# Banded attention scores: the correction product over all 128 rows, and the fp32 scores of two heads in turn

## The chip, the cores and the metric

One core of a Trainium2 chip runs the whole program. The metric is the time of one execution on the device in microseconds: a median of 1695.29 us over three runs (1690.89 to 1697.64).

## What is computed

The reference is an encoder trunk of two layers over 512 tokens of 1024 features, all in float32. The first layer mixes tokens by attention with 16 heads of 64 features, the second by a state-space layer; after each comes a gated feed-forward of 2816 hidden features, and a norm ends the trunk. The change concerns the attention alone. It has three groups of queries, keys and values (a window of 128 tokens; 512 with dilation 4; 2048 with dilation 16), whose outputs are weighted by a softmax over their log-sum-exps:

```python
scores = jnp.einsum('brnqhe,brnkhe->brnhqk', qb, kw, preferred_element_type=jnp.float32)
scores = jnp.where(valid[None, None, :, None], scores + bias[None, None, None], NEG_INF)
m = jnp.max(scores, axis=-1, keepdims=True)
p = jnp.exp(scores - m)
den = jnp.sum(p, axis=-1, keepdims=True)
o = jnp.einsum('brnhqk,brnkhe->brnqhe', p, vw.astype(jnp.float32))
o = o / den.transpose(0, 1, 2, 4, 3, 5)
lse = (m + jnp.log(den))[..., 0].transpose(0, 1, 2, 4, 3)
...
weights = jax.nn.softmax(jnp.stack(lses, axis=0), axis=0)
o = jnp.sum(weights[..., None] * jnp.stack(outs, axis=0), axis=0)
```

## The kernel before

**Main products.** A weight block of 128 x 1024 is loaded by a DMA that SP issues (L91) three blocks ahead, and split into a high part by ACT (L111) and the rest by DVE (L112). A product of 512 columns is then three matmuls for each of 8 feature tiles (high by high, high by low, low by high) in PSUM (`gemm_a`, L735; for the values of the second and third group `emit_v`, L836, with 256 columns). A pair p of heads (2p and 2p + 1, on partitions 0 to 63 and 64 to 127) has seven such units: q1, k1, q2, k2, q3, k3 and v1. `plan` gives their order: pairs one after another, with a block of values before pairs 1, 3, 5 and 7.

**The steps of attention** are put between the matmuls of later units. `bg.span` gets a list of steps, each with a cost in ns, and the main work of the span in ns (216 a matmul). After each feature tile, `bg.tick` adds 648 times the ratio of the two sums (and 1.02) to a credit, and issues the next step when the credit has reached half its cost, which is then taken off. So the order on each engine's queue is fixed when the program is written. The lists come from `A`, `W`, `B`, `mix`, `scores` and `values` (L998 to L1018): for an even head h, `scores(h)` has the four score steps of h, and those of h + 1 among the weighting steps of h; `values(h)` has the transposes and the products with the values of both heads. `spans` (L1020) sets them over the units: pairs 0, 1, 3 and 5 get scores and values over the q/k units of the pair behind them, pairs 2, 4 and 6 get their scores over a block of values, and `A(14)` lies over the very last unit. Head 15 and the values of the last pair stand in `tailp` (L1062), whose first five steps are issued while the operand of the output projection is made (`xo`, ACT L1059 and DVE or POOL L1060), and the rest between the matmuls of that projection (L1079, L735).

**Score steps.** `sc1(h, bp)` (L866) makes the banded scores of two blocks of 128 queries against 256 keys each. The keys' tile of a head holds their high part in one half of the partitions and their low part in the other; QA or QB holds the queries' high part in both halves. So one matmul over 128 rows (L880) gives high by high and high by low; a second (L881) adds the queries' low part QL by the keys' high part, over the head's 64 rows alone:

```python
nc.tensor.matmul(ps[:, j, :], QQ[:, b * 128:(b + 1) * 128], kap(KK), start=True, stop=False)
nc.tensor.matmul(ps[:, j, :], QL[rows, b * 128:(b + 1) * 128], kap(KK[rows]), start=False, stop=True)
```

`sc2(h, rp)` (L889) makes the scores of the other two groups, in fp32, over the head's 64 rows: four matmuls of 128 columns (L898, L899). Each step writes one bank of the PSUM pool `pss`, which has two. DVE reads a step's result with two instructions that add the distances, scale and take the maximum (L884 or L902); ACT then takes the exponential (L913).

**Weighting and values.** `weigh` has four parts (16 small copies on POOL, L925, then DVE and ACT); `tr` transposes on PE (L954, L959), with the result split by ACT and DVE (L962, L963); `pv` multiplies with the values (L978, L989) and ends a head with t1 (ACT L992, DVE L993, L994).

Where the parts of the queries are made (`qk_out`), QL is one tile per pair with two buffers; DVE writes its halves at L782 and L783. At the start of the program two small tiles `grow` receive the norms' gains by DMA, `sqd` takes squares of the input, of which only the sums are used, and t1 has a tile of 64 partitions with two buffers.

Of the kernel before, what the change touches and what calls it, by code (L numbers as in the profile page):

```python
# [13 lines left out]
P = 128  # L14
S = 512
# [11 lines left out]
def consts():  # L27
    """Tables that depend on shapes alone."""
    i = np.arange(128)
    q = np.arange(128)  # L30
    # natural tile: partition (r, i'), token 128 b + 4 i' + r
    d1 = np.full((128, 3, 2, 4, 32), BIG, np.float32)
    starts = {0: (0, 16), 1: (16, 48), 3: (80, 96)}
    for v, b in enumerate((0, 1, 3)):
        tq = 128 * b + 4 * (q % 32) + q // 32
        for T in range(2):
            for r in range(4):
                j = np.arange(32)
                tk = 4 * (starts[b][T] + j) + r
                dist = np.abs(tq[:, None] - tk[None, :])  # L40
                ok = dist <= 64
                if b == 0 and T == 0:
                    ok = ok & (j < 16)[None, :]
                if b == 3 and T == 1:
                    ok = ok & (j >= 16)[None, :]
                d1[:, v, T, r, :] = np.where(ok, dist, BIG)
    di = np.abs(i[:, None] - i[None, :])
    d2 = np.where(di <= 64, 4 * di, BIG)
    d3 = np.where(di % 4 == 0, 4 * di, BIG)
    dist = np.concatenate([d1.reshape(128, 768), d2, d3], axis=1).astype(np.float32)  # L50
    qs = np.zeros((128, NH // 2), np.float32)
    for p in range(NH // 2):
        qs[:64, p] = -1.0 / (8.0 * SLOPES[2 * p])
        qs[64:, p] = -1.0 / (8.0 * SLOPES[2 * p + 1])
    part = np.arange(128)
    dmask = (part[:, None] % 32 == np.arange(16)[None, :]).astype(np.float32)
    return np.concatenate([dist, qs, np.eye(128, dtype=np.float32), dmask], axis=1).astype(np.float32)
# [9 lines left out]
def fv(ap):  # L67
    return ap.bitcast(F32)


class WStream:
    """Weight blocks of [128, <=1024], loaded ahead and split into two f32r parts."""
# [22 lines left out]
    def split_to(self, n):  # L95
        nc = self.k.nc
        while self.ns <= min(n, len(self.units) - 1):
            w = self.raw.pop(self.ns)
            a, b = w.shape[1], w.shape[2]
            hi = self.pool.tile([P, 1024], F32R, tag="whi", name="whi")  # L100
            lo = self.pool.tile([P, 1024], F32R, tag="wlo", name="wlo")
            hv, lv = (t[:, 0:a * b] for t in (hi, lo))
            wv = w.rearrange("p a b -> p (a b)")
            if self.ns in self.swap:
                # columns (g, c) become (c, g)
                src = w.rearrange("p a (g c) -> p a c g", c=16)
                h4, l4 = (t.rearrange("p (a c g) -> p a c g", a=a, c=16) for t in (hv, lv))
                nc.scalar.activation(out=h4, in_=src, func=ACTF.Copy)
                self.lo_engine.tensor_tensor(out=l4, in0=src, in1=fv(h4), op=ALU.subtract)
            else:  # L110
                nc.scalar.activation(out=hv, in_=wv, func=ACTF.Copy)  # L111
                self.lo_engine.tensor_tensor(out=lv, in0=wv, in1=fv(hv), op=ALU.subtract)  # L112
            self.hl[self.ns] = tuple(t.rearrange("p (a b) -> p a b", a=a) for t in (hv, lv))
            self.ns += 1
# [9 lines left out]
class Bg:  # L124
    """Work put between the matmuls of the main products."""
# [27 lines left out]
class Cycle:  # L153
    """Tiles from several pools in turn."""
# [10 lines left out]
class Later:  # L165
    """An engine whose instructions are written down, to be issued in parts."""
# [9 lines left out]
class Tables:  # L176
    """What the state-space layer needs of its parameters, on the chip: rows are (direction, state)."""
# [15 lines left out]
    def scratch(self, n, cols):  # L193
        """A tile that is needed only while the parameters are worked out."""
        if not self.spare:
            tag, size = self.tags.pop()
            t = self.pool.tile([P, size], F32, tag=tag, name="sp_" + tag)
            self.spare = [t[:, i:i + 512] for i in range(0, size - 511, 512)]
        return self.spare.pop()[:, 0:cols]
# [4 lines left out]
    def cmul(self, eng, o_r, o_i, ar, ai, br, bi, t, neg=False):  # L204
        """o = a * b; neg gives -imag."""
# [8 lines left out]
    def exp(self, x, out, em1=None):  # L214
        """exp(x), and exp(x) - 1, to float32's accuracy."""
# [22 lines left out]
    def sincos(self, x, s, c, cm1):  # L238
        """sin, cos and cos - 1 of x, [128, 448]."""
# [46 lines left out]
    def params(self):  # L286
# [24 lines left out]
        # powers 1 .. 8 of lambda  # L311
# [6 lines left out]
        # f = (lambda - 1) / a  # L318
# [22 lines left out]
        for i in range(2):  # L341
# [4 lines left out]
            # the other direction from the far end  # L346
# [45 lines left out]
    def bc(self, w, i, g0):  # L392
        """powers [l, i, g] as (g, l, c)"""
# [3 lines left out]
    def ch(self, x):  # L397
        """channels (g, c) as (g, l, c)"""
# [73 lines left out]
    def store_e(self, T, s):  # L472
        # row (lam, c) of the block Toeplitz matrix is a window of the band at 16 lam
# [5 lines left out]
    def pieces(self):  # L479
        """(share of the time, what to issue)"""  # L480
# [32 lines left out]
def build(tc, a, out):  # L513
# [6 lines left out]
    # ---- weights in the order in which they are used  # L520
# [41 lines left out]
    # row 256 * t2 + 128 * tp + 64 * gp + s of w_glu: partition (tp, s), block (t2, gp)  # L562
# [13 lines left out]
    with ExitStack() as ctx:  # L576
# [19 lines left out]
        def norm_tile(pool, i, m, src_psum=None):  # L596
            """Parts of (gain * h)^T for feature tile m."""
# [9 lines left out]
        # of -y / 2 as an integer, the bits of a first guess at 1 / sqrt(y)  # L607
        GUESS = 1597463007.0 - 2.0 ** 22 - 2.0 ** 30

        def rs_col(ms, r):  # L610
            """r = rsqrt(ms / D + eps), [128, 4]"""
# [17 lines left out]
        # =================== attention ===================  # L629
# [12 lines left out]
        grow = [ap_.tile([8 * n, P], F32, name=f"grow{n}") for n in (1, 3)]  # L642
# [14 lines left out]
        # a first use of the exponential, so that its table is there  # L657
# [21 lines left out]
        def squares(c, act):  # L679
            for r in range(4):  # L680
                sqd = ap_.tile([P, 256], F32, tag="sqd", name="sqd")
# [63 lines left out]
        def emit_qk(p, lo_, hi_):  # L745
            if lo_ == 0:
                qk[p] = {}
            for kind in ("q1", "k1", "q2", "k2", "q3", "k3", "v1")[lo_:hi_]:
                if p == 0 and kind == "q1":
                    # the scale of the tokens comes later  # L750
# [12 lines left out]
        def qk_out(p, kind, ps):  # L763
            if True:
# [9 lines left out]
                elif kind == "q1":  # L774
                    t = ap_.tile([P, S], F32, tag="tq", name="tq", bufs=2)
                    nc.vector.tensor_tensor(out=br(t), in0=rb(ps), in1=rb(rsB), op=ALU.mult)
                    QA, QB, QL = (ap_.tile([P, S], F32R, tag=n, name=n, bufs=2) for n in ("QA", "QB", "QL"))
# [4 lines left out]
                    nc.vector.tensor_tensor(out=QL[0:64], in0=t[0:64], in1=fv(QA[0:64]), op=ALU.subtract)  # L782
                    nc.vector.tensor_tensor(out=QL[64:128], in0=t[64:128], in1=fv(QB[64:128]), op=ALU.subtract)  # L783
# [82 lines left out]
        def sc1(h, bp):  # L866
# [4 lines left out]
            QQ = (QA, QB)[e]  # L871
            ps = pss.tile([P, 2, 256], F32, tag="s", name="sps")
            for j in range(2):
                b = 2 * bp + j
                i0, step = win[b]
                rows = slice(64 * e, 64 * e + 64)
# [4 lines left out]
                nc.tensor.matmul(ps[:, j, :], QL[rows, b * 128:(b + 1) * 128], kap(KK[rows]), start=False, stop=True)  # L881
# [7 lines left out]
        def sc2(h, rp):  # L889
            c = head(h)  # L890
            p, e = h // 2, h % 2
            rows = slice(64 * e, 64 * e + 64)
            q = qk[p]
            ps = pss.tile([P, 2, 256], F32, tag="s", name="sps")
            for j in range(2):
                r = 2 * rp + j
                cs = slice(r * 128, (r + 1) * 128)
                nc.tensor.matmul(ps[:, j, 0:128], q["q2"][rows, cs], q["k2"][rows, cs], start=True, stop=True)  # L898
                nc.tensor.matmul(ps[:, j, 128:256], q["q3"][rows, cs], q["k3"][rows, cs], start=True, stop=True)  # L899
            for j in range(2):  # L900
                r = 2 * rp + j
                nc.vector.tensor_tensor_reduce(out=c.P2[:, r, :], in0=ps[:, j, :], in1=dist23,  # L902
                                               scale=-SLOPES[h], scalar=-3e38, op0=ALU.add, op1=ALU.max,
                                               accum_out=c.st[:, 4 + r:5 + r])
            fin(c, c.P2, 2 * rp, 4)

        # st: 0:8 m, 8:16 den, 16:24 partner m, 24:32 partner den (halves swapped), 32:40 -m, 40:48 work
# [8 lines left out]
        def weigh(h, part):  # L916
# [9 lines left out]
            elif part == 1:  # L926
                # par[.., k] holds the partner values of the other kind: slot k of par goes with slot 1-k of own
# [38 lines left out]
        def pv(h, t):  # L966
# [23 lines left out]
            if t == 1:  # L990
                t1 = ap_.tile([64, 2, 256], F32, tag="t1", name="t1", bufs=2)
# [6 lines left out]
        def A(h):  # L998
            return [(750, lambda: sc1(h, 0)), (880, lambda: sc2(h, 0)), (750, lambda: sc1(h, 1)), (880, lambda: sc2(h, 1))]
# [8 lines left out]
        def mix(x, y):  # L1008
            """the steps of two heads in turn"""
# [3 lines left out]
        def scores(h):  # L1013
            w, x = W(h), A(h + 1)
            return A(h) + [w[0], x[0], w[1], x[1], w[2], w[3], x[2], x[3]]
# [16 lines left out]
        def sq_add(m, acc):  # L1032
            """acc += h^2 for feature tile m."""
# [35 lines left out]
        for m in range(4):  # L1069
            wl = ws.get(ahead=min(1, 3 - m))  # L1070
            ps = (psg, psg, pss, pss)[m].tile([P, S], F32, tag="ggss"[m], name="aps")
            if m == 0:
                # the second parts of the operand come last
# [24 lines left out]
        # tables of the state-space layer, built between the products  # L1098
# [28 lines left out]
        # =================== feed-forward ===================  # L1127
        def ffn_in(hp, ep, psp, X, st, lo_, hi_, off, hid, pool_mult):
# [16 lines left out]
            for j in range(lo_, hi_):  # L1145
                gp = psp.tile([P, S], F32, tag="f", name="gps2")
                if st["rB"] is None and not late:
                    # the last feature tile of the input and the sums of squares come late
# [41 lines left out]
        for half in range(2):  # L1190
            ffn_in(hp0, e0, psf, Y, st, half * HALF, (half + 1) * HALF, half * HALF, hid, False)
            for m in range(KT):
# [6 lines left out]
                else:  # L1199
                    # from here on tokens lie as (l, j), t = 8 j + l  # L1200
# [15 lines left out]
        # =================== state-space layer ===================  # L1216
# [28 lines left out]
        def s_rho(T):  # L1245
            # decay per step, none across the ends of a group
# [189 lines left out]
        # =================== second feed-forward and last norm ===================  # L1436
# [102 lines left out]
```

## Time and profile before

| | |
|---|---|
| Median of three runs | 1695.29 us (1690.89 to 1697.64) |
| Profiled execution, first to last instruction | 1689.3 us |
| What the median has above that span | 6.0 us |
| Instructions | 22568 |
| Matmul engine (PE) busy | 1586.0 us, 94% |
| Weight loads (PEld) busy | 1287.1 us, 76% |
| DVE, ACT, POOL busy | 1015.5, 654.9, 528.7 us |
| Mean granted TensorE clock | 0.977 |

The profile has one execution. PE's busy time overlaps itself: a matmul's recorded length runs past the start of the next, so what a matmul costs is read from the distance of two starts. A weight load has a record of its own. "Idle before" an instruction names what ended the idle time, by the semaphore that came last; "issue" means that the profile shows no such cause. The attention stage runs to about 592 us, with the last unit of pair 7 at about 549 us.

### The profile page before, as it was taken

The numbers are of one execution on the slowest core, as the hardware profiler recorded it, in microseconds if no ns is written. First come the engines' busy times: TensorE is split into PE (matmuls) and PEld (weight loads), VectorE is DVE, ScalarE is ACT, GpSimd is POOL, SyncE is SP. The second block draws the span as 40 slices with busy tenths as digits, with TensorE's granted clock in tenths as the row PEclk, the third lists the DMA queues.
The fourth block names the chain that finished last, engine by engine and source line by source line (L and its number), as shares of the span: only waits on it lengthen the run. The fifth ranks groups of instructions, "written<-read, shape, count | busy, mean of one in ns | idle before, by whom it ended". The sixth has DMA issues, their size and how long they took to land. (4 is left out here: it accounts for less than half of the span.)

```text
span 1689.3 us, 22568 instructions
## 1 busy us (share of the span) xinstructions
PE 1586.0 (94%) x8428; PEld 1287.1 (76%) x8428; DVE 1015.5 (60%) x1714; ACT 654.9 (39%) x1148; POOL 528.7 (31%) x784
## 2 busy tenths in 40 slices
PE   8999999999999889988988889888699999999997
PEld 6877887887888668866666667667578888888886
DVE  6466565555655678887777785568945434433223
ACT  5355454454444523343444444422133323332222
POOL 0011011020120340298887996345412110111010
PEclk9999999999999999999999998989899999999999
DMA  6322222222222033345655544657723333233332
GB/s 186 91 63 63 63 78 60 75 63 75 75 58 80 26 84 100 97 126 162 176 145 168 143 127 147 226 165 242 205 76 94 94 100 100 88 89 107 105 100 63
DMA packets 278669, 185.17 MB, mean 110 GB/s; under 512 B 39424, under 2 KB 260768, under 8 KB 276512
## 3 DMA queue, kind: packets, MB, share of 16 engines
q1 hardware_dynamic: 278128, 183.13, 36.9%
q8 instruction: 66, 1.08, 0.3%
q10 hardware_dynamic: 432, 0.60, 0.1%
q14 instruction: 43, 0.35, 0.1%
HBM read 154.34 MB, written 27.26 MB: 108 GB/s over the span
## 5 line engine op out<-in xcount | busy, mean ns | idle before, releaser
L112 DVE TENSOR_TENSOR wlo<-wraw,whi 128x1024 fp32r<-128x1024 f32 (+1 forms) x234 | 304.0, 1302 | 184.5 <-ACT whi L111 183.1
L111 ACT ACTIVATE whi<-wraw 128x1024 fp32r<-128x1024 f32 x238 | 241.3, 1018 | 248.4 <-PE ops L1498 76.0
L735 PE MATMUL gps<-xhi,whi 128*128 128x512 f32 x792 | 322.7, 407 | 0.0
L735 PE MATMUL gps<-xhi,wlo 128*128 128x512 f32 x792 | 312.2, 394 | 0.8 <-DVE wlo L112 0.8
L735 PE MATMUL gps<-xlo,whi 128*128 128x512 f32 x792 | 311.7, 394 | 0.5 <-DVE xlo L602 0.5
L925 POOL COPY st<-st 32x4 f32<-32x4 f32 x256 | 66.0, 258 | 484.5 <-ACT P L913 475.8
L735 PEld LDWEIGHTS gps<-xhi,wlo 128*128 128x128 f32 x792 | 149.4, 189 | 34.8 <-DVE wlo L112 1.2
L735 PEld LDWEIGHTS gps<-xhi,whi 128*128 128x128 f32 x792 | 149.6, 189 | 31.6 <-issue 1.5
L735 PEld LDWEIGHTS gps<-xlo,whi 128*128 128x128 f32 x792 | 149.9, 189 | 26.7 <-DVE xlo L602 0.8
L735 PE MATMUL ups<-xhi,whi 128*128 128x512 f32 x352 | 140.9, 400 | 0.0
L735 PE MATMUL ups<-xhi,wlo 128*128 128x512 f32 x352 | 138.7, 394 | 1.0 <-DVE wlo L112 1.0
L735 PE MATMUL ups<-xlo,whi 128*128 128x512 f32 x352 | 138.6, 394 | 0.0
L913 ACT ACTIVATE P<-P,st 128x256 f32<-128x256 f32 x128 | 64.1, 501 | 88.3 <-DVE st L910 88.2
L1137 POOL TENSOR_TENSOR u<-u,g 128x512 f32<-128x512 f32 x22 | 28.4, 1290 | 214.1 <-DVE u L1135 202.2
L735 PEld LDWEIGHTS ups<-xhi,wlo 128*128 128x128 f32 x352 | 66.9, 190 | 15.8 <-DVE wlo L112 1.5
L735 PEld LDWEIGHTS ups<-xhi,whi 128*128 128x128 f32 x352 | 67.0, 190 | 15.6 <-issue 2.3
L1134 ACT ACTIVATE g<-g 128x512 f32<-128x512 f32 x44 | 27.8, 631 | 129.2 <-DVE g L1133 129.2
L735 PEld LDWEIGHTS ups<-xlo,whi 128*128 128x128 f32 x352 | 67.0, 190 | 13.2
L963 DVE TENSOR_TENSOR PT<-ptp,PT 128x512 fp32r<-128x512 f32 x64 | 44.0, 690 | 54.5 <-ACT PT L962 54.1
L836 PE MATMUL vps<-whi,xhi 128*128 128x256 f32 x256 | 75.1, 293 | 0.0
L735 PE MATMUL fps<-hh,whi 128*128 128x512 f32 x176 | 72.7, 413 | 0.0
L836 PE MATMUL vps<-wlo,xhi 128*128 128x256 f32 x256 | 72.2, 282 | 0.0
(319 smaller groups left out, 3312.2 us busy)
## 6 DMA issues: line engine op xcount, KB each, us to landing
wraw<-in_w_ffn_in SPq DMA_DIRECT2D x88, 512.0 KB, 3.8
wraw<-in_w_qkv SPq DMA_DIRECT2D x72, 512.0 KB, 3.6
wraw<-in_w_ffn_out SPq DMA_DIRECT2D x38, 512.0 KB, 4.0
BD<-B SPq DMA_DIRECT2D x16, 512.0 KB, 3.4
TinD<-Tt SPq DMA_DIRECT2D x16, 512.0 KB, 2.6
Ti<-TinD SPq DMA_DIRECT2D x8, 1024.0 KB, 7.2
Bt<-BD SPq DMA_DIRECT2D x8, 1024.0 KB, 8.1
wraw<-in_w_glu SPq DMA_DIRECT2D x64, 128.0 KB, 3.9
```

The source lines that it names most:

```text
L111: nc.scalar.activation(out=hv, in_=wv, func=ACTF.Copy)
L112: self.lo_engine.tensor_tensor(out=lv, in0=wv, in1=fv(hv), op=ALU.subtract)
L735: nc.tensor.matmul(dst, w[:, kt, :], x, start=(start and kt == ks[0] and j == 0), stop=(stop and kt == ks[-1] and j == 2))
L836: nc.tensor.matmul(ps[rp][:, r % 2, :], x, w[:, kk, :], start=(kt == 0 and j == 0 and r % 2 == 0), stop=(kt == 7 and j == 2 and r % 2 == 1))
L913: nc.scalar.activation(out=Pt[:, j, :], in_=Pt[:, j, :], func=ACTF.Exp, bias=st[:, 32 + off + j:33 + off + j], accum_out=st[:, 8 + off + j ...
L925: nc.gpsimd.tensor_copy(par[32 * z:32 * z + 32, y, :, :], own[32 * y:32 * y + 32, z, :, :])
L963: nc.vector.tensor_tensor(out=PT[:, 1, :], in0=ps, in1=fv(PT[:, 0, :]), op=ALU.subtract)
L1134: nc.scalar.activation(out=g, in_=g, func=ACTF.Silu)
L1137: eng.tensor_tensor(out=u, in0=u, in1=g, op=ALU.mult)
```

## The change

- The correction product of the banded scores (L881) uses all 128 rows. There are four QL tiles, made once: two for pairs in turn, two for the heads of a pair. Each is zero in the other head's half; POOL clears these halves at the start. DVE writes the head's own half as before.
- `sc2` takes a pair in place of a head. It takes both banks of `pss`, and issues the matmuls of the two heads in turn: q2 by k2 of head 0, of head 1, q3 by k3 of head 0, of head 1. DVE's readings follow, head by head.
- The lists: an even head's has sc1, sc2 of the pair, sc1, sc2 of the pair; an odd head's has its two sc1 alone. Costs are 600 for sc1 and 1200 for the pair's sc2, where they were 750 and 880.
- `grow`, `sqd` and t1 lie in one tile t1x of 128 partitions: t1 of a head in the head's 64 partitions, with one buffer. Comments and docstrings are taken out.

```diff
+        t1x = ap_.tile([P, 2, 256], F32, name="t1x")
+        t1f = t1x.rearrange("p a b -> p (a b)")
+        grow = [t1f[0:8, 0:128], t1f[0:24, 128:256]]
+        QLs = [[ap_.tile([P, S], F32R, name=f"QL{i}{e}") for e in range(2)] for i in range(2)]
+        for i in range(2):
+            for e in range(2):
+                nc.gpsimd.memset(QLs[i][e][64 * (1 - e):64 * (1 - e) + 64].bitcast(F32), 0.0)
...
-                sqd = ap_.tile([P, 256], F32, tag="sqd", name="sqd")
+                sqd = t1f[:, 256:512]
...
-                    nc.vector.tensor_tensor(out=QL[0:64], in0=t[0:64], in1=fv(QA[0:64]), op=ALU.subtract)
-                    nc.vector.tensor_tensor(out=QL[64:128], in0=t[64:128], in1=fv(QB[64:128]), op=ALU.subtract)
+                    nc.vector.tensor_tensor(out=QL[0][0:64], in0=t[0:64], in1=fv(QA[0:64]), op=ALU.subtract)
+                    nc.vector.tensor_tensor(out=QL[1][64:128], in0=t[64:128], in1=fv(QB[64:128]), op=ALU.subtract)
...
-                nc.tensor.matmul(ps[:, j, :], QL[rows, b * 128:(b + 1) * 128], kap(KK[rows]), start=False, stop=True)
+                nc.tensor.matmul(ps[:, j, :], QL[:, b * 128:(b + 1) * 128], kap(KK), start=False, stop=True)
...
+        def sc2(p, rp):
+            cc = [head(2 * p + e) for e in range(2)]
             q = qk[p]
+            pp = [pss.tile([P, 2, 256], F32, tag="s", name="sps") for e in range(2)]
             for j in range(2):
                 r = 2 * rp + j
                 cs = slice(r * 128, (r + 1) * 128)
+                for i, (nq, nk) in enumerate((("q2", "k2"), ("q3", "k3"))):
+                    for e in range(2):
+                        rows = slice(64 * e, 64 * e + 64)
+                        nc.tensor.matmul(pp[e][:, j, 128 * i:128 * i + 128], q[nq][rows, cs], q[nk][rows, cs],
+                                         start=True, stop=True)
+            for e, c in enumerate(cc):
+                for j in range(2):
...
+                fin(c, c.P2, 2 * rp, 4)
...
-                t1 = ap_.tile([64, 2, 256], F32, tag="t1", name="t1", bufs=2)
+                t1 = t1x[64 * e:64 * e + 64]
...
-            return [(750, lambda: sc1(h, 0)), (880, lambda: sc2(h, 0)), (750, lambda: sc1(h, 1)), (880, lambda: sc2(h, 1))]
+            s = [(600, lambda: sc1(h, 0)), (600, lambda: sc1(h, 1))]
+            t = [(1200, lambda i=i: sc2(h // 2, i)) for i in range(2)]
+            return s if h % 2 else [s[0], t[0], s[1], t[1]]
...
-            return A(h) + [w[0], x[0], w[1], x[1], w[2], w[3], x[2], x[3]]
+            return A(h) + [w[0], x[0], w[1], x[1], w[2], w[3]]
```

## Rows read from the trace of the kernel before

**Rows 1.** The page: span, and busy us (share) with instructions of each engine.

```profile
span 1689.3 us, 22568 instructions
...
PE 1586.0 (94%) x8428; PEld 1287.1 (76%) x8428; DVE 1015.5 (60%) x1714; ACT 654.9 (39%) x1148; POOL 528.7 (31%) x784
```

**Rows 2.** Busy time by stretches: PE, PEld, DVE, ACT, POOL, clock, DMA share, GB/s.

```profile
78.00:158.00 80.00, 80.00 (x387) 61.96 (x385) 50.47 (x146) 43.60 (x102) 12.43 (x50) 1.00 0.23 66
...
549.00:563.00 14.00, 10.47 (x42) 6.90 (x41) 11.59 (x28) 7.13 (x20) 10.76 (x21) 0.83 0.01 2
...
560.00:562.00 2.00, 2.00 (x9) 1.78 (x8) 2.00 (x3) 0.00 (x1) 2.00 (x3) 0.50 0.00 0
```

**Rows 3.** Timeline of PE, one step of banded scores: start us, us, instruction.

```profile
134.69 0.40 PE L735 MATMUL gps<-xhi,wlo 128*128 128x512 f32 x1
134.92 0.28 PE L880 MATMUL sps<-KA,QA 128*128 128x256 f32 x1
135.13 0.38 PE L881 MATMUL sps<-KA,QL 64*128 64x256 f32 x1
...
135.76 0.38 PE L881 MATMUL sps<-KA,QL 64*128 64x256 f32 x1
136.07 0.50 PE L735 MATMUL gps<-xhi,whi 128*128 128x512 f32 x1
136.41 0.39 PE L735 MATMUL gps<-xlo,whi 128*128 128x512 f32 x1
```

**Rows 4.** Timeline of PE, products of the values with 256 columns.

```profile
76.05 0.28 PE L836 MATMUL vps<-wlo,xhi 128*128 128x256 f32 x1
...
77.37 0.29 PE L836 MATMUL vps<-whi,xhi 128*128 128x256 f32 x1
```

**Rows 5.** Timeline of PEld, the load for the correction product.

```profile
135.13 0.18 PEld L881 LDWEIGHTS sps<-KA,QL 64*128 64x128 f32 x1 [0.25 <-issue]
```

**Rows 6.** Timeline of PE, one step of fp32 scores of one head.

```profile
80.85 0.40 PE L735 MATMUL gps<-xhi,wlo 128*128 128x512 f32 x1
81.17 0.48 PE L898 MATMUL sps<-k,q 64*128 64x128 f32 x2
81.50 0.38 PE L899 MATMUL sps<-k,q 64*128 64x128 f32 x2
...
81.95 0.38 PE L899 MATMUL sps<-k,q 64*128 64x128 f32 x2
82.26 0.50 PE L735 MATMUL gps<-xhi,whi 128*128 128x512 f32 x1
82.60 0.39 PE L735 MATMUL gps<-xlo,whi 128*128 128x512 f32 x1
```

**Rows 7.** The scores' PSUM tile by instruction: ns min/median/max, first and last start.

```profile
L898 PE MATMUL sps<-k,q x128: 268/272/579, 81.2 to 561.4; 64*128 64x128 f32 x128
...
L884 DVE CUSTOM_DVE_ANT_0 P<-sps,cst x64: 409/418/425, 81.6 to 563.3; 128x256 f32<-128x256 f32 x64
...
L880 PE MATMUL sps<-KA,QA x32: 278/334/386, 78.4 to 545.0; 128*128 128x256 f32 x32
```

**Rows 8.** Timeline of PE, state-space stage: products for two column halves in turn.

```profile
1116.51 0.70 PE L1242 MATMUL V<-U,Ti 128*64 128x64 f32 x18
```

**Rows 9.** Timeline of DVE, the readings of the banded step of rows 3.

```profile
136.96 0.42 DVE L884 CUSTOM_DVE_ANT_0 P<-sps,cst 128x256 f32<-128x256 f32 x1
...
137.30 0.42 DVE L884 CUSTOM_DVE_ANT_0 P<-sps,cst 128x256 f32<-128x256 f32 x1
```

**Rows 10.** Waits of PE, 548 to 600 us: us in total, times, longest.

```profile
PE aps L1079 <- ACT ohi L1059: 2.9, 2, 1.9
```

**Rows 11.** Timeline of PE, the second fp32 step of head 15.

```profile
560.16 0.79 PE L898 MATMUL sps<-k,q 64*128 64x128 f32 x2
...
562.16 0.79 PE L1079 MATMUL aps<-ohi,whi 128*128 128x512 f32 x1
```

**Rows 12.** Timeline of POOL, its first instruction on the program's data.

```profile
10.43 2.39 POOL L112 TENSOR_TENSOR wlo<-wraw,whi 128x1024 fp32r<-128x1024 f32 x1 [9.99 <-ACT whi L111]
```

More of the change, by code (lines that the diff above doesn't have):

```diff
@@ L640, in build @@
         pso = atp.enter_context(tc.tile_pool(name="pso", bufs=1, space=PSUM))
-        grow = [ap_.tile([8 * n, P], F32, name=f"grow{n}") for n in (1, 3)]
+        t1x = ap_.tile([P, 2, 256], F32, name="t1x")
[5 more added lines that the diff above has]
+                nc.gpsimd.memset(QLs[i][e][64 * (1 - e):64 * (1 - e) + 64].bitcast(F32), 0.0)
         xv = a["x"][0].rearrange("(i r) d -> i r d", r=4)
@@ L776, in qk_out @@
                     nc.vector.tensor_tensor(out=br(t), in0=rb(ps), in1=rb(rsB), op=ALU.mult)
-                    QA, QB, QL = (ap_.tile([P, S], F32R, tag=n, name=n, bufs=2) for n in ("QA", "QB", "QL"))
+                    QA, QB = (ap_.tile([P, S], F32R, tag=n, name=n, bufs=2) for n in ("QA", "QB"))
+                    QL = QLs[p % 2]
                     nc.scalar.activation(out=QA[0:64], in_=t[0:64], func=ACTF.Copy)
@@ L870, in sc1 @@
             KK = qk[p]["K"][e]
-            QQ = (QA, QB)[e]
+            QQ, QL = (QA, QB)[e], QL[e]
             ps = pss.tile([P, 2, 256], F32, tag="s", name="sps")
@@ L875, in sc1 @@
                 i0, step = win[b]
-                rows = slice(64 * e, 64 * e + 64)
                 def kap(t):
@@ L887, in sc1 @@
             fin(c, c.P1, 2 * bp, 0)
[L889 to L892, printed above, removed]
+        def sc2(p, rp):
+            cc = [head(2 * p + e) for e in range(2)]
             q = qk[p]
-            ps = pss.tile([P, 2, 256], F32, tag="s", name="sps")
+            pp = [pss.tile([P, 2, 256], F32, tag="s", name="sps") for e in range(2)]
             for j in range(2):
@@ L897, in sc2 @@
                 cs = slice(r * 128, (r + 1) * 128)
[L898 to L905, printed above, removed]
+                for i, (nq, nk) in enumerate((("q2", "k2"), ("q3", "k3"))):
[5 more added lines that the diff above has]
+                for j in range(2):
+                    r = 2 * rp + j
+                    nc.vector.tensor_tensor_reduce(out=c.P2[:, r, :], in0=pp[e][:, j, :], in1=dist23,
+                                                   scale=-SLOPES[2 * p + e], scalar=-3e38, op0=ALU.add, op1=ALU.max,
+                                                   accum_out=c.st[:, 4 + r:5 + r])
+                fin(c, c.P2, 2 * rp, 4)
         def fin(c, Pt, j0, off):
```

## The prediction

> **What bounds the kernel now.** I read the page first: the matmul engine (PE) is busy 94% of 1689.3 us, DVE 60%, and no other engine comes near [rows 1]. An average over stages decides nothing, so the busy time by stretches comes next: in the attention stage PE is busy 80.00 of 80.00 us at a granted clock of 1.00 (its upper level, 2.4 GHz), with DVE at 50.47; only the end of that stage, 549 to 563 us, has PE holes (10.47 of 14.00, clock 0.83) [rows 2]. So up to 549 us every microsecond of PE issue that goes, goes from the time, unless a wait takes its place.
>
> The timeline of PE then shows what a scores step costs. Look at the distances between starts, not at the durations, which overlap. Main products of 512 columns start 0.23 us apart (134.69 to 134.92). In the step of banded scores, L880 (128 rows) and L881 (64 rows) alternate: the four start from 134.92, 135.13 to 135.76, and the next main product at 136.07, whose successor is also late, by 0.34 instead of 0.23 [rows 3]. These are 256-column products, and 256-column products that all use 128 rows start 0.12 apart (11 of them from 76.05 to 77.37) [rows 4]. The weight load shows why: that of L881 starts at 135.13, together with its own product and after 0.25 us of "issue", not during the product before [rows 5]. Each change between 128 and 64 rows costs PE about 0.2 us. The fp32 step has such a change at either end alone: 0.32 before it (80.85 to 81.17), 0.31 after its last row and 0.34 behind the first main product; within it two instructions take 0.22 to 0.23, so 0.112 each [rows 6].
>
> **The correction over 128 rows (L881).** A step now costs 136.07 - 134.92 = 1.15, plus 0.34 - 0.23 = 0.11 for the late successor: 1.26 us. With four products of equal shape it is 4 x 0.12 = 0.48. Gain 0.78 a step. The trace has 32 + 32 products of each line, so 64 / 2 = 32 steps (the 32 of the even heads are shown) [rows 7]; 30 of them (heads 0 to 14 and no others) lie before 549 us, where PE is full: 30 x 0.78 = **23.4 us**. I take that 0.12 [rows 4] since operand shapes and types agree; the far end is no gain at all, if the hidden part were due to something other than the rows.
>
> **The fp32 scores of two heads in turn.** Now one head's step costs 0.09 at entry, 1.09 inside (81.17 to 82.26) and 0.11 at the exit: 1.29 us, of which 8 x 0.112 = 0.90 is products [rows 6]; the 128 recorded products of a line are two for each of its 64 calls [rows 7]. 30 steps before 549 us make 38.7. After the change 16 steps, all before that point, hold 16 instructions each; those of head e read partitions 64 e to 64 e + 63 and write a PSUM bank of their own. What two halves do side by side is not in this trace. One end: they follow one another, 1.29 + 8 x 0.112 = 2.19 a step, 35.0 in all, a gain of 3.7. The other end: they run together and the step costs 1.29 as for one head, 20.6 in all, a gain of 18.1. The nearest row is that of products for two column halves in turn: 18 of 64 columns lie within 0.70 us, under 0.04 each [rows 8], where 0.112 per 128 columns would make 0.056 each, 1.0 us in all. They overlap there, so I take **18.1**.
>
> **The wait that the change adds.** The scores' PSUM pool has two banks. The old steps used one in turn; the new fp32 step takes both, so its second head waits for DVE to have read the banded step before it. The steps are placed by credit: the pieces of a span of 36,288 ns of main work now add up to 26,400 (28,120 before), a ratio of 0.742, 481 for each tick of three products; that puts sc1, sc2, sc1, sc2 behind ticks 1, 3, 5, 7. So from the start of sc1 to that of the second head's products pass 0.48 + 6 x 0.23 + 0.09 = 1.95 us. DVE comes to it late: for pair 1 sc1 starts at 134.92, the second reading ends at 137.30 + 0.42 = 137.72 [rows 3, 9], 2.80 later: PE stands 0.85 us, and all main products with it, as they queue behind on the same engine. Pairs 3, 5 and 7 are placed alike: 4 x 0.85 = 3.4. Pair 0 is the worst: from 78.4 to 81.6 + 0.34 + 0.42 = 82.4 are 4.0 us, a stall of 2.0 (the first start of either line, and the distance and length of two readings) [rows 7, 9]. Pairs 2, 4 and 6 lie over a V block, with six ticks of three 0.12 products between the two steps (0.48 + 2.16 + 0.09 = 2.73 against 2.80): 0.1 each. Together 5.7, taken as **6 us lost**; bounds 2 (DVE earlier than now) and 12 (each of the 32 bank handovers another 0.2). The following steps find their bank read: a step's own four readings take 4 x 0.38 = 1.5 us (two take 137.72 - 136.96) [rows 9], and the next step is 2 ticks, 1.4 us, and a step's length behind.
>
> **The end of the stage.** Head 15's fp32 scores leave 549 to 563 us for the full part. There PE waits for the parts of the operand (ACT ohi, 2.9 us in two waits) [rows 10], so what ran before 559 us hides behind that and I count nothing; but the second step of head 15 ran from 560.16 to 562.16 at the lower clock, 0.50 [rows 2, 11], 2.0 us on the path, and with it out the weights of head 15 start earlier. I take **3 us gained**; ends 0 and 6 (the 3.5 us of holes and those 2.0).
>
> **Edits at nothing.** Four memsets on POOL: its first work is at 10.43 us after 9.99 us idle [rows 12], and a clear of 64 x 512 can hardly take over half of the 2.39 us of that 128 x 1024 split: 4.8 us for four, which would show once at the start without that cover. QL stays at two writes a pair on DVE. The shared scratch tile: gains' rows and squares use different columns, t1 different rows for the two heads of a pair; 0; were the squares made to wait for the gains' load, part of the first 10.43 us [rows 12] would come again, half of it, 5 us, as an estimate. The list without sc2 for odd heads puts w2 and w3 right before the transposes that read them; the credits still leave some five ticks, 3.5 us, for 2 us of DVE work.
>
> **Sum.** 23.4 + 18.1 + 3 - 6 = 38.5; I take 37.5, one off for the first of 16 instructions that has no partner in each step (16 x 0.112 = 1.8, half of it). From the profiled span of 1689.3 that leaves 1651.8; the median of the runs, 1695.29, is 6.0 over that span, so the prediction is **1657.8 us**.
>
> **Rivals.** *The halves do not overlap.* For it: no row here shows two row halves; loads 0.112 apart are as well explained by the load of 128 columns as by the product. Against: the overlap of the column halves [rows 8]. Gain 23.4 + 3.7 + 3 - 6 = 24.1: 1671. The Trainium skill (TensorE: Matmul & The Clock Gate, section on LDWEIGHTS) says that a load takes its columns over 1.2 GHz, the same for 32 rows as for 128, 107 ns here; if loads went one by one, its rule would give this rival's 1671, and the column halves [rows 8], each product of which has a load of its own, speak against it.
>
> *Each change of half costs like a change of rows.* 8 changes a step at 0.1 more than now, 0.8 us: 2.99 a step, 47.8 in all, a loss of 9.1 against 38.7: 23.4 - 9.1 + 3 - 4 = 13, 1682. Nothing in the trace shows it. The Trainium skill (TensorEngine Tiling (Array Packing), section Key Properties) has a drain for a change of tiling mode, not of the tile alone, by which this would not occur; no run here shows it yet.
>
> *The correction does not gain*: load and product stay apart for another reason than the rows, and 18.1 + 3 - 6 = 15 remain: 1680.
>
> *Slower: the bank handover decides.* Place: the two-bank pool, 32 handovers of the 16 fp32 steps. If DVE were as late each time as for pair 0, 32 x 2.0 = 64 us are lost against 44.5 gained: 1715. It breaks even at 1.4 us a handover. For it: pair 0's lag. Against: the other lags are 0.85 and 0.1, and DVE has 37% free there [rows 2].
>
> **How the numbers follow.** The forecast 0.64 (its own range 1649 to 1667: stalls 2 to 12, tail 0 to 6); no overlap 0.19; costly change of half 0.06; no gain of the correction 0.05; handover 0.06. 0.5% of 1695 is 8.5 us, about what runs of this kernel can tell. The first four cases lie over it: faster 0.94. Of the last, half falls within 0.5% and half beyond: 0.03 and 0.03. The range, 1648 to 1676, takes in the first two, 0.83, less the outer ends of the first.
>
> **What would show it.** In the changed profile: starts of banded products 0.12 apart and no late main product behind them; fp32 products of the two heads starting in twos, 16 within about 0.9 us (1.8 for the second case, over 2.5 for the third); PE waits for DVE's reading of the scores at the second head's products, some 2 us in pair 0 and 0.85 in 1, 3, 5, 7; no sc2 behind the end of the last q/k unit. The number is wrong if PE's busy share in the attention stage falls below 95%, or if the halves follow one another.

## The result and the profile after

The changed kernel takes **1681.99 us** (median of four runs, 1681.01 to 1683.88) beside 1693.23 for the kernel before in the same comparison: a ratio of 0.993, 95% interval 0.9912 to 0.9948. It is faster by about 11 us, not by 37, and the time lies above the predicted range.

The page of the changed kernel answers to [rows 1]:

```profile
span 1682.1 us, 22587 instructions
...
PE 1557.8 (93%) x8428; PEld 1278.0 (76%) x8428; DVE 1014.1 (60%) x1714; ACT 653.7 (39%) x1148; POOL 524.8 (31%) x788
```

PE is busy 28 us less, and the span is only 7 shorter. The busy time by stretches shows where they went (changed kernel; columns as in [rows 2]):

```profile
78.00:158.00 80.00, 73.17 (x400) 60.27 (x399) 47.75 (x134) 41.38 (x99) 12.64 (x48) 0.96 0.20 60
161.00:166.00 5.00, 1.05 (x6) 0.57 (x5) 3.87 (x10) 2.99 (x7) 4.28 (x13) 0.95 0.04 9
166.00:169.00 3.00, 3.00 (x10) 2.52 (x9) 1.10 (x3) 1.55 (x5) 0.00 (x0) 0.51 0.49 164
```

The stretch that was full, 80.00 of 80.00 at clock 1.00, now has 73.17 at 0.96: 91%, under the 95% that the prediction named as its own refutation. In the second line PE is busy for 1.05 of 5 us; in the third the granted clock is 0.51, the lower of the two levels (1.2 GHz), right behind that hole.

Who PE waits for, in the list of its waits from 78 to 520 us (us in total, times, longest). For the kernel before this list is empty; for the changed kernel:

```profile
PE ptp L970 <- DVE P L951: 16.0, 4, 4.1
PE sps L908 <- DVE st L892: 5.0, 7, 1.5
```

The second line is the bank handover that was forecast. The first was not forecast at all: the transposes of the weighted scores wait four times some 4 us for DVE.

**The new steps themselves** do what the prediction took. Timeline of PE, changed kernel (start us, us, instruction): a fp32 step of two heads, then a banded step and a fp32 step that waits:

```profile
88.63 0.40 PE L742 MATMUL gps<-xhi,wlo 128*128 128x512 f32 x1
88.96 1.16 PE L908 MATMUL sps<-k,q 64*128 64x128 f32 x16
90.05 0.50 PE L742 MATMUL gps<-xhi,whi 128*128 128x512 f32 x1
90.39 0.39 PE L742 MATMUL gps<-xlo,whi 128*128 128x512 f32 x1
...
139.96 0.28 PE L887 MATMUL sps<-KA,QA 128*128 128x256 f32 x1
140.07 0.28 PE L889 MATMUL sps<-KA,QL 128*128 128x256 f32 x1
140.19 0.28 PE L887 MATMUL sps<-KA,QA 128*128 128x256 f32 x1
140.31 0.28 PE L889 MATMUL sps<-KA,QL 128*128 128x256 f32 x1
140.43 0.39 PE L742 MATMUL gps<-xhi,whi 128*128 128x512 f32 x1
140.66 0.39 PE L742 MATMUL gps<-xlo,whi 128*128 128x512 f32 x1
...
141.90 0.48 PE L908 MATMUL sps<-k,q 64*128 64x128 f32 x2
142.80 1.16 PE L908 MATMUL sps<-k,q 64*128 64x128 f32 x14 [0.42 <-DVE st L892]
```

The four banded products start 0.12 apart, and the second main product behind them comes 0.23 after the first: no late one. From the first of the sixteen fp32 products to the next main product pass 90.05 - 88.96 = 1.09 us, as much as for the eight of one head [rows 6]. The last two lines are a handover, 0.90 from the first product of head 0 to the fourteen that follow; with it the step takes 1.99 us. The idle time in brackets, 0.42, is less than the 0.90, since it counts only from the recorded end of the product before.

The pair's second fp32 step has a handover as well. First PE, then DVE, which comes late to the second banded step because it waits for ACT:

```profile
147.73 0.48 PE L908 MATMUL sps<-k,q 64*128 64x128 f32 x2
148.97 1.16 PE L908 MATMUL sps<-k,q 64*128 64x128 f32 x14 [0.75 <-DVE st L892]
...
147.54 0.69 DVE L828 TENSOR_TENSOR V<-vtp,V 128x512 fp32r<-128x512 f32 x1 [1.89 <-ACT V L827]
148.15 0.41 DVE L892 CUSTOM_DVE_ANT_0 P<-sps,cst 128x256 f32<-128x256 f32 x1
```

**The hole.** PE again, at the transposes of pair 1:

```profile
161.33 0.40 PE L742 MATMUL gps<-xhi,wlo 128*128 128x512 f32 x1
165.68 1.11 PE L970 MATMUL ptp<-cst,P 128*128 128x128 f32 x4 [3.95 <-DVE P L951]
166.45 0.78 PE L742 MATMUL gps<-xhi,whi 128*128 128x512 f32 x1
167.02 0.63 PE L742 MATMUL gps<-xlo,whi 128*128 128x512 f32 x1
167.45 0.63 PE L742 MATMUL gps<-xhi,wlo 128*128 128x512 f32 x1
```

and DVE at that time, from the reading of the finished k1 unit (L795) to the weighting steps w2 (L947) and its scaling (L951):

```profile
159.89 0.74 DVE L795 SCALAR_TENSOR_TENSOR tq<-gps,cst,rsB 128x512 f32<-128x512 f32 x1
161.67 0.69 DVE L799 TENSOR_TENSOR KA<-tq,KA 64x512 fp32r<-64x512 f32 x1 [1.03 <-ACT KA L797]
162.39 0.69 DVE L800 TENSOR_TENSOR KB<-tq,KB 64x512 fp32r<-64x512 f32 x1
163.40 1.25 DVE L112 TENSOR_TENSOR wlo<-wraw,whi 128x1024 fp32r<-128x1024 f32 x1 [0.33 <-ACT whi L111]
164.57 0.22 DVE L947 TENSOR_TENSOR st<-st 128x4 f32<-128x4 f32 x2
...
165.27 1.14 DVE L951 TENSOR_SCALAR P<-P,st 128x256 f32<-128x256 f32 x4
```

In the kernel before, the same two steps stand ahead of that reading (L787 there):

```profile
153.31 0.23 DVE L936 TENSOR_TENSOR st<-st 128x4 f32<-128x4 f32 x2
...
154.02 1.14 DVE L940 TENSOR_SCALAR P<-P,st 128x256 f32<-128x256 f32 x4
155.08 0.75 DVE L787 SCALAR_TENSOR_TENSOR tq<-gps,cst,rsB 128x512 f32<-128x512 f32 x1
```

A unit of main products has eight ticks. From the order of the instructions, w2 came behind tick 16 before, the last tick of a unit; it now comes behind tick 17, past the unit's end, and the transposes behind tick 22 instead of 24. Being one tick later puts w2 on DVE's queue behind everything that the end of a unit issues: the reading, two differences that wait for ACT's roundings (L797, L798), and the next block's split, which waits for ACT's part (L111). It is 0.74 + 0.69 + 0.69 + 1.25 = 3.4 us of DVE work and, with the waits, 164.57 - 159.89 = 4.7 us. PE gives the transposes five ticks after w2, 3.5 us; DVE begins w2 3.2 us after the last main product before them. The other three waits of this kind are those of pairs 0, 3 and 5, whose steps have the same places.

### The profile page after: what moved, and what is told of

The parts are those of the page before. It is cut to its first block, busy times and chain, and to the rows that moved or that the text cites. A ratio compares the mean times of both kernels' runs of the same rounds, so it can differ in the third digit from the quotient of the medians.

```text
span 1682.1 us, 22587 instructions
## 1 busy us (share of the span) xinstructions
PE 1557.8 (93%) x8428; PEld 1278.0 (76%) x8428; DVE 1014.1 (60%) x1714; ACT 653.7 (39%) x1148; POOL 524.8 (31%) x788
## 5 line engine op out<-in xcount | busy, mean ns | idle before, releaser
L111 ACT ACTIVATE whi<-wraw 128x1024 fp32r<-128x1024 f32 x238 | 241.5, 1019 | 260.5 <-PE ops L1511 76.3
L936 POOL COPY st<-st 32x4 f32<-32x4 f32 x256 | 62.1, 243 | 475.8 <-ACT P L924 351.3
L742 PE MATMUL fps<-hh,wlo 128*128 128x512 f32 x176 | 71.3, 405 | 1.5 <-DVE wlo L112 1.5
```

The lines of the kernel that those rows point to most:

```text
L742: nc.tensor.matmul(dst, w[:, kt, :], x, start=(start and kt == ks[0] and j == 0), stop=(stop and kt == ks[-1] and j == 2))
L936: nc.gpsimd.tensor_copy(par[32 * z:32 * z + 32, y, :, :], own[32 * y:32 * y + 32, z, :, :])
```

## The experiments

Medians come with the ratio to the kernel before on the same chip (1696.7 for the first four, 1694.2 for the next two, 1695.1 for the rest). The kernel before has from 1693.2 to 1696.7 over the groups, so a difference of two medians from different groups is good to some 3 us; what a part is worth is better read from the stage. "The stage" is the time from the first product of the values to the first of the output projection. The first starts of those instructions (ns min/median/max, first and last start) give it; for the kernel before, 551.1 - 54.3:

```profile
L836 PE MATMUL vps<-whi,xhi x256: 279/282/388, 54.3 to 497.3; 128*128 128x256 f32 x128
...
L1079 PE MATMUL aps<-ohi,whi x7: 474/498/793, 551.1 to 563.9; 128*128 128x512 f32 x7
```

and for the changed kernel, 545.7 - 56.3:

```profile
L844 PE MATMUL vps<-whi,xhi x256: 277/282/388, 56.3 to 491.8; 128*128 128x256 f32 x128
...
L1092 PE MATMUL aps<-ohi,whi x7: 458/522/775, 545.7 to 557.8; 128*128 128x512 f32 x7
```

The table splits it further. "Banded" is the sum over the 30 banded steps of heads 0 to 14, "fp32" that over their fp32 steps (30 by head, 16 by pair), each step from its first product to the instruction behind it, waits inside the step included. "Idle" is what the list of PE's waits has in the stage before the output projection's first product. The rest of the stage is main work and the other steps.

| kernel | median us | stage us | banded | fp32 | idle of PE |
|---|---|---|---|---|---|
| before | 1693.2 | 496.9 | 34.5 | 32.6 | 0 |
| after | 1682.0 | 489.4 | 14.3 | 26.6 | 21.5 |
| w2 a place earlier | 1675.0 | 482.7 | 14.3 | 26.6 | 17.4 |
| empty steps | 1667.8 | 476.7 | 14.5 | 29.9 | 11.3 |
| correction alone | 1671.1 | 473.3 | 14.4 | 32.6 | 0 |
| heads one after the other | 1682.0 | 492.2 | 14.7 | 29.0 | 15.3 |
| costs 500 and 1000 | 1665.3 | 471.1 | 14.6 | 28.9 | 8.7 |
| spaced | 1656.2 | 464.7 | 14.7 | 18.8 | 5.9 |
| more space | 1660.5 | 468.9 | 14.6 | 26.0 | 7.0 |
| spaced, one after the other | 1661.4 | 468.2 | 14.6 | 27.0 | 2.1 |
| spaced, 64 rows | 1672.9 | 482.8 | 35.0 | 18.0 | 1.3 |

Sixteen fp32 steps without a handover would take 16 x 1.09 = 17.4 us in turn, so 9.2 of the 26.6 of the changed kernel are handover.

Both kernels were run and profiled once more, unchanged: 1694.4 and 1683.9 us, with stages of 496.6 and 489.2. So a stage repeats to 0.3 us, while the whole spans of the kernel before differ by 3.3. A profile shows one execution; three of them lay over their medians by 7.5 us (empty steps), 4.0 (heads one after the other) and 2.1 (64 rows).

What was asked: is it the place of w2 in the order that costs the missing 26 us (37.5 forecast, 11.2 measured), or something in the new steps, the handover of the banks or the issue in turn itself?

**w2 one place earlier in the list**, with steps and costs as they are:

```diff
-            return A(h) + [w[0], x[0], w[1], x[1], w[2], w[3]]
+            return A(h) + [w[0], x[0], w[1], w[2], x[1], w[3]]
```

> The changed kernel with one swap in the list of steps: the third weighting part w2 now comes before the odd head's second banded step, so that it is issued behind tick 16, the last of the unit, and not behind tick 17, after the reading of k1 and the next weight split. The first transposes stay at tick 22. Theory A (w2 slid past the end of the unit and stands on DVE behind that unit's work): the four waits of PE of 4.1 us for w2, and the 1.5 us at the lower clock behind each, go: 20 to 22 us less than the changed kernel's 1682, so 1660 to 1662. Theory B (the transposes are too close behind w3, wherever w2 stands): the four waits stay, 1680 to 1684.

Measured: 1674.95 us, 0.988 [0.9858, 0.9902]. Its waits from 78 to 520 us:

```profile
PE ptp L965 <- DVE PT L974: 11.9, 4, 3.1
PE sps L908 <- DVE st L892: 5.0, 7, 1.5
```

The wait of the first transposes for w2 is gone, with w2 back behind tick 16. But the banded step of the odd head went past the unit's end in its place (tick 18); its readings and exponentials, and w3 with them, come late on ACT and DVE, and the third group of transposes (L965) now waits some 3 us each time for DVE's copy of the group before. Moving one step moves the hole; it took away 7 us. It confirms that the place of w2 matters, not that it is all.

**The ticks of before, by empty steps** that cost the credit but issue nothing:

```diff
-            return A(h) + [w[0], x[0], w[1], x[1], w[2], w[3]]
+            n = (880, lambda: None)
+            return A(h) + [w[0], x[0], w[1], n, w[2], w[3], x[1], n]
```

> The changed kernel with two empty steps of cost 880 where the odd head's fp32 steps were. By the credits w2 stays behind tick 17, past the end of the unit, but the first transposes move from tick 22 to 24, where they are in the kernel before. Theory A: the four waits shrink only by the two ticks, 1.4 us each, from 4.1 to about 2.7: some 6 to 8 us less, 1674 to 1677. Theory B (distance from w3 to the transposes): the waits go as a whole, 1660 to 1663.

Measured: 1667.76 us, 0.984 [0.9815, 0.9866]; 14 us of the 26 came back, between what the theories gave. With transposes at tick 24 again their wait is 2.2 us in place of 16.0, although w2 still stands at tick 17; the handover takes 7.1. The list also puts the odd head's second banded step behind w3, which takes its readings from DVE's queue ahead of w2, so this run does not show what the two ticks alone are worth.

**The correction over 128 rows alone**, with the fp32 steps, lists and costs of before:

```diff
...
-            t = [(1200, lambda i=i: sc2(h // 2, i)) for i in range(2)]
-            return s if h % 2 else [s[0], t[0], s[1], t[1]]
+            return [(750, lambda: sc1(h, 0)), (880, lambda: sc2(h, 0)), (750, lambda: sc1(h, 1)), (880, lambda: sc2(h, 1))]
...
-            return A(h) + [w[0], x[0], w[1], x[1], w[2], w[3]]
+            return A(h) + [w[0], x[0], w[1], x[1], w[2], w[3], x[2], x[3]]
```

> The correction product over 128 rows alone: fp32 scores by head, with the lists and costs of the kernel before, so every step stands where it stood. Sum of the prediction: 30 x 0.78 = 23.4 us less than before, with no new wait at w2 and none at the banks: 1693 - 23 = 1670, to 1667 if the end of the stage gains as well. Rival (the rows are not what separates load and product, or the freed PE time is eaten by waits elsewhere): 1688 to 1694.

Measured: 1671.12 us, 0.9852 [0.9836, 0.9868]: this half of the change is faster than the whole. The stage is 496.9 - 473.3 = 23.6 us shorter, against a term of 23.4. The list of PE's waits from 78 to 520 us is empty, as in the kernel before, and PE is full:

```profile
78.00:158.00 80.00, 80.00 (x421) 65.35 (x420) 53.42 (x158) 46.18 (x111) 13.44 (x50) 1.00 0.24 69
```

**The two heads one after the other** in the joint fp32 step, by the order of the loops:

```diff
+            for e in range(2):
...
                 for i, (nq, nk) in enumerate((("q2", "k2"), ("q3", "k3"))):
-                    for e in range(2):
```

> The changed kernel with the fp32 matmuls of head 0 first and those of head 1 behind them, all else alike. If the two halves overlap only when issued in turn, a step takes 8 x 0.112 = 0.9 us more, 14 us in 16 steps, less up to 0.9 us in those steps in which the second head waited for its bank anyway (some 6 of them): 1688 to 1696. If the order made no difference: 1682.

Measured: 1681.99 us, 0.9919 [0.99, 0.9937], against 0.993 [0.9912, 0.9948] for the changed kernel; that the two medians agree to the hundredth is chance. Taken alone they would say that issue in turn is worth nothing. The stage is 2.8 us longer, and the split shows why it is no more: a step without a handover takes 1.64 us instead of 1.09 (lines further down, from the spaced order), which makes 16 x 1.64 = 26.2 of the 29.0, 8.8 more than 17.4; but the second head's products come later and find their bank read, so that the handover falls from 9.2 to 2.8 (idle time from 5.0 to 0.9 in the list). What PE saves at one place it waits for at the next.

**Smaller costs**, which give a smaller sum and so another ratio and other ticks, with nothing else changed:

```diff
-            s = [(600, lambda: sc1(h, 0)), (600, lambda: sc1(h, 1))]
-            t = [(1200, lambda i=i: sc2(h // 2, i)) for i in range(2)]
+            s = [(500, lambda: sc1(h, 0)), (500, lambda: sc1(h, 1))]
+            t = [(1000, lambda i=i: sc2(h // 2, i)) for i in range(2)]
```

> The changed kernel with two numbers of the credit alone: 500 for a banded step and 1000 for a pair's fp32 step, in place of 600 and 1200. By the credits the odd head's second banded step then stands behind tick 14 and w2 behind tick 16, both before the end of the unit (15 and 17 in the changed kernel; swapping the two, in the first experiment, freed w2 but put the banded step past the end). Theory A (a step issued just past the end of a unit stands on DVE and ACT behind that unit's reading and the next weight split, some 4 us): the waits at the transposes go, 17 to 20 us less than the changed kernel: 1662 to 1665. Theory C (without the odd head's fp32 steps between, DVE and ACT have not caught up whatever the place): waits of 2 us and more stay at one of the transposes of each pair, 1672 or more.

Measured: 1665.32 us, 0.9826 [0.9795, 0.9857]. This is the plainest test: the same instructions in the same lists, w2 behind tick 16 and the transposes behind 21, so still five ticks apart, and the wait at the transposes is gone from the list:

```profile
PE sps L908 <- DVE st L892: 7.4, 8, 1.5
PE sps L887 <- DVE st L913: 1.1, 3, 0.4
```

Two numbers in the plan are worth 17 us. What remains is the handover.

**Space for the handover too**: costs of 300 and 800, and empty steps between a pair's first banded step and its fp32 step.

```diff
...
-            return s if h % 2 else [s[0], t[0], s[1], t[1]]
+            return s if h % 2 else [s[0], (800, lambda: None), t[0], s[1], (600, lambda: None), t[1]]
```

> As the run before, and the pair's fp32 steps moved away from the banded steps by empty steps (costs 300 and 800, with empty ones of 800 and 600 between): behind ticks 1, 4, 5, 7, so that DVE has read the banded step when the second head wants its bank. Theory A and the bank handover as predicted: the eight waits for DVE's reading, 5.7 us in all and about 2 more of fp32 products that stand apart, fall to 2 or less: 4 to 6 us less than the run before, 1657 to 1661. If the handover costs nothing because other waits would take its place: the same as the run before.

Measured: **1656.24 us** (1655.76 to 1657.98), 0.978 [0.9756, 0.9805]: faster than both kernels, 26 us below the changed one. Its waits:

```profile
PE sps L887 <- DVE st L913: 3.9, 4, 1.2
PE ptp L970 <- DVE P L951: 1.2, 4, 0.3
PE sps L908 <- DVE st L892: 0.8, 1, 0.8
```

The handover at the second head's products is down from 5.0 to 0.8; 3.9 of it came back at the banded step behind the fp32 step, which now finds both banks unread.

**More space** (fp32 steps at 300, banded ones at 300 and 200, empty steps of 1100, 500 and 300, and one of 200 behind w3) was to take away the rest.

> The spaced version with empty steps set finer: by the credits banded and fp32 steps behind ticks 1, 4, 6, 7, the odd head's banded steps behind 11 and 13, w2 behind 15, the transposes behind 21. The waits left in the spaced version (three of 1.4 us for the reading of an fp32 step at the second banded step, four of 0.5 us for w2) should go: 4 to 6 us less than its 1656, 1650 to 1653. If the credits only move the waits: 1655 to 1658.

A miss: 1660.49 us, 0.9798 [0.978, 0.9816]; the intervals overlap, but the stage is 4.2 us longer than in the spaced kernel. The ticks moved over the blocks of values as well: L908 waits 4.3 us in four handovers, three of them (1.2 each) over those blocks, and L887 1.6. With two banks and steps this close, space taken at one place is missing at another.

**The parts again, in the spaced order**, where PE hardly waits. Heads one after the other:

> The spaced version with the fp32 matmuls of head 0 first and those of head 1 behind them. With hardly any wait at the banks left, the step's length decides: 1.44 us against 0.89 from the first to the last start in the two kernels with waits, 0.55 us in 16 steps: 8.8 us more than the spaced version's 1656, about 1665. If the order of issue is worth nothing: 1656.

Measured: 1661.43 us, 0.9808 [0.9789, 0.9827], 5.2 over the spaced kernel on another chip; the stage is 3.5 longer. The fp32 steps take 27.0 - 18.8 = 8.2 us more, 0.55 in each of fifteen (the first of pair 0 waits in both), and more than half of it comes back elsewhere (the idle time falls from 5.9 to 2.1). A step without waits there, timeline of PE:

```profile
86.84 1.71 PE L908 MATMUL sps<-k,q 64*128 64x128 f32 x16
88.48 0.50 PE L742 MATMUL gps<-xhi,whi 128*128 128x512 f32 x1
```

It is 1.64 us long instead of 1.09.

The correction over 64 rows again, with the issue in turn kept:

```diff
...
-                nc.tensor.matmul(ps[:, j, :], QL[:, b * 128:(b + 1) * 128], kap(KK), start=False, stop=True)
+                nc.tensor.matmul(ps[:, j, :], QL[rows, b * 128:(b + 1) * 128], kap(KK[rows]), start=False, stop=True)
```

> The spaced version with the correction product over the head's 64 rows again: the fp32 scores in turn alone, without the waits. 32 steps cost 0.78 us more: 25 us more than 1656, 1681, which leaves 13 us below the kernel before for the turn alone. If the two parts shared their gain (the saved changes of rows counted twice): nearer to 1670.

Measured: 1672.9 us, 0.9862 [0.9839, 0.9886], better than expected. In the stage, against 496.9, the correction alone gains 23.6 us, the spaced turn alone 14.1, and both together 32.2. They fall 5.5 short of adding up, and the waits account for most of it: with the longer banded step PE reaches them later (1.3 us of idle time against 5.9).

## Why the prediction was wrong

The sum of 37.5 had four terms and a list of edits at nothing. By its own steps:

- **Correction, 23.4: right.** 23.6 in the stage when made alone; 0.12 between products and no late successor, so both costs came from the change of rows.
- **In turn, 18.1: right.** Sixteen products take 1.09 us, the entry is 0.33 (88.63 to 88.96) and the next main product late by 0.11 as before: 1.29 a step, as for one head. The last 1 us taken off the sum was not needed. "The halves do not overlap" wanted 2.19 a step and "each change of half" 2.99; both fall. The Trainium skill (TensorEngine Tiling (Array Packing), section Key Properties) has tiles that load and multiply independently, and a drain for a change of mode alone; the 1.09 agrees, and so does the 0.33 where the rows do change. The Trainium skill (TensorE: Matmul & The Clock Gate, section on LDWEIGHTS) has a load take its columns over 1.2 GHz, by which sixteen loads of 128 columns one by one would take 1.7 us, an estimate. They did not go one by one: each is recorded with 0.18 to 0.19 us, and the sixteen start within 0.78 us, in twos.
- **Handover, 6 lost: 9.2.** What was worked out came as it was worked out: pair 0 loses 2.0 (its first step takes 3.09 us for 1.09), pairs 1, 3 and 5 lose 0.90 at the first step and pair 7 0.78, for 0.85; pairs 2, 4 and 6 nothing, for 0.1. What failed is "The following steps find their bank read": in pairs 1, 3 and 5 the second fp32 step loses 1.23 as well, 3.7 in all, since DVE waits for ACT ahead of its reading. It was no "slower".
- **End of the stage, 3 gained:** 4.4. From the first product of the output projection to the first with its last feature tile (L1093, now L1106) the kernel before takes 591.3 - 551.1 = 40.2 us and the changed one 581.5 - 545.7 = 35.8.
- **Edits at nothing: the failed step**, and in it the sentence on the list: "the credits still leave some five ticks, 3.5 us, for 2 us of DVE work". The five ticks are right (17 to 22). The 2 us are w2's own work. What stands ahead of it on DVE was not counted, 4.7 us that it meets by being placed one tick past the end of a unit. Five ticks are enough otherwise: with costs 500 and 1000 the transposes follow w2 by five as well, and do not wait. The ratio of 0.742, used to place the handovers, would have given w2's tick as well; it was not carried on to the end of the list.

The price: by the sum the stage was to shrink by 23.4 + 18.1 - 6 - 1 = 34.5 us, and it shrank by 7.5, so 27.0 are missing. The four holes, from the start of the last main product to that of the transposes and less the usual 0.23, make 16.6. Behind each hole the clock is at its lower level for about 3 us of products, in pair 0 for 5, with main products 0.42 to 0.57 apart instead of 0.23; that is some 15 us in the stage, of which 7.4 are lost. Together 24.0. The handover has 3.2 more than its 6, and the 1 us of the first instructions was not lost: 24.0 + 3.2 - 1 = 26.2, and head 15's steps at the stage's very end take 0.7 more (2.75 for 2.04). The spaced kernel checks it: holes of 1.9, no stretch at the lower level, 1.4 of handover, and 4.5 that it waits at banded steps instead, so 16.6 + 7.4 + 9.2 - 1.9 - 1.4 - 4.5 = 25.4, and its stage is 489.4 - 464.7 = 24.7 shorter.

The medians, 1682.0 for 1657.8, are 24.2 apart, where the stage and its end make 27.0 - 1.4 = 25.6. That they come so close is in part luck, since the profiled spans, 1682.1 for 1651.8, are 30.3 apart: the stage starts 2.0 later, and the rest of the program takes 2.6 more, where two profiles of the kernel before differ by 3.8. The 6.0 that the prediction put between span and median was no constant either; the other profiles have 1.8 to the time of their own execution, and the profiled one of the kernel before was fast. It is also chance that 1682 was the number of the rival "each change of half" and 1680 that of "the correction does not gain": the 1.09 a step and the 23.6 rule both out.

The cover that the prediction leaned on, DVE with 37% free [rows 2], says nothing of one queue's order at one moment; and the sign it set for its own failure, PE under 95%, is the one that came.

One thing stays open: the first product of the values starts at 54.3 and 54.0 in two profiles of before, at 55.1 to 56.9 in ten of kernels with the change in whole or part, and at 54.4 in the one with 64 rows, which has the same memsets and shared tile. POOL's clears (0.73 to 2.93 us) are over long before its first work at 10.96, so they are not it; no run isolates this.

## What to carry to other kernels

When a change makes the steps of an interleaved plan shorter, work out the new place of every step behind them, down to the last consumer, and for each ask what stands ahead of it on the engine that serves it; the cheap step that slipped past a unit's end cost 24 us here, more than half of the work saved. Read a part's worth in its own steps before reading it in the time: the loop order is worth 8 to 9 us in the fp32 steps, but 3 in the stage, because PE waits the rest away. And where costs in a plan are only weights, try a few: here two of them gave more than the change itself.

## What the runs showed of the hardware

- Two fp32 products on the two row halves, from two heads and into two banks, cost PE no more than one: 1.09 us for sixteen in turn, as for eight [rows 6].
- Not issued in turn, sixteen take 1.64, not 1.09 + 0.90 = 1.99. In the step shown, the trace's record of the product that waits for the second head's bank starts at 87.396, 0.33 us before the last one of the first head at 87.725: PE overlaps products of the second head with the last of the first without being told to.
- A hole of 4 us in PE's work costs more than itself: at 166 to 169 us the granted clock is 0.51, and the four holes of the changed kernel cost 7.4 us so. A shorter hole can do the same, but did not each time: in the kernel with costs 500 and 1000, one of four waits of 1.5 us was followed by main products at the lower pace, the one of pair 5:

```profile
399.44 1.16 PE L908 MATMUL sps<-k,q 64*128 64x128 f32 x14 [1.46 <-DVE st L892]
...
400.92 0.63 PE L742 MATMUL gps<-xlo,whi 128*128 128x512 f32 x1
401.35 0.63 PE L742 MATMUL gps<-xhi,wlo 128*128 128x512 f32 x1
```
